# A sparse 3x3 convolution on one core: all cast loads queued at the start, fixed output tiles

## The chip, the cores and the metric

The kernel runs on one core of a Trainium2 chip. The metric is the device time of one execution in microseconds, the median of several runs. The core has five engines that matter here: TensorE (PE) multiplies, VectorE (DVE), ScalarE (ACT) and GpSimd (POOL) work on tiles, and SyncE (SP) issues transfers. Transfers run on 16 DMA engines. Those that SP issues stand in queue q1, those that POOL issues in queue q0.

## The reference

The input `x` has 16 images of 64 channels with 64 x 64 points, the weight has 128 output channels, 64 input channels and 3 x 3 taps, about 90% of them zero. All data are 32-bit floats. What is computed is an ordinary convolution with a border of zeros:

```python
x_pad = np.pad(x, ((0, 0), (0, 0), (pad, pad), (pad, pad)), mode='constant')
output = np.zeros((batch, c_out, h, w), dtype=np.float32)
for b, co, ci, kh, kw in ...:
    if weight[co, ci, kh, kw] != 0:
        output[b, co] += weight[co, ci, kh, kw] * x_pad[b, ci, kh:kh+h, kw:kw+w]
```

The output is 33.55 MB, twice the 16.78 MB of `x`.

## The kernel before

The zeros are not used; the kernel is dense. Two images make a pair: their 2 x 64 channels fill the 128 partitions, and PE runs the two images' matmuls on the two halves of its rows (K = 64 each). There are eight pairs, p = 0 to 7, and eight input tiles `xs[p]` in bf16, all in SBUF for the whole run, so no load ever waits for a buffer.

**Loads.** The weight and the first half of pair 0 (`x_head`) come as plain 32-bit loads on SP's queue; casts on DVE and ACT make bf16 of them. All other input comes through POOL's queue as DMAs that cast to bf16 while they move (`load`, L68, and L63 for the second half of pair 0). Pairs 1 to 3 and the first 24 rows of pair 4 are issued at the start (`EARLY`, `CUT`). The rest is issued later: after the last block of pairs 1 to 5 the program issues, in turn, the rest of pair 4, pair 5, pair 6, and pair 7 in two halves (`LATER`). Since POOL works its instructions off in order, such a load goes out when POOL has done the `s` of that block.

**Compute.** A pair has four blocks of 16 rows. All blocks but the first of pair 0 go through `twos`: POOL adds neighbouring rows into a tile `s` (L169), PE makes a product `shared` from it, ACT copies that from PSUM to `pc` (L176), PE makes a product for the even and one for the odd rows (L150), and DVE adds `pc` to each of them and writes `o` (L183, four writes of 128 x 512 a block). The first block of pair 0 goes through `direct`. Each of PE's products takes two tiles of the PSUM pool, which has eight, one bank each.

**Stores.** The output of a pair is one tile `both` of 4 MB, from a pool with three buffers (`bufs=3`); `o[0]` and `o[1]` are its two images. When a pair is done, SP issues one store for it (L207). Pair 7 goes out in two stores, after block 1 and after block 3 (L205). DVE's first write of pair p + 3 waits until the store of pair p has landed, because it takes that buffer. After the store of pair 1, SP issues five loads of one number each into a tile `spare` (L211), which nothing reads. DMAs of SP take eight semaphores in turn; before a DMA takes a semaphore again, SP waits for the DMA that had it before. With the five small ones, pair 3's store follows pair 0's on the same semaphore, pair 4's follows pair 1's, and pairs 5 to 7 follow the small ones.

The program fixes the order of every engine's instructions as written (`manual_schedule`).

Of the kernel before, what the change touches and what calls it, by code (L numbers as in the profile page):

```python
# [8 lines left out]
FP32 = mybir.dt.float32  # L9
# [2 lines left out]
SUB = mybir.AluOpType.subtract  # L12

BLOCKS = {p: "TTTT" for p in range(8)}
BLOCKS[0] = "DTTT"  # L20


G0, G1, G2, G21, G01 = range(5)
# [4 lines left out]
def kernel(  # L28
# [6 lines left out]
    nc = tc.nc  # L35

    B, C_IN, H, W = x.shape
    C_OUT, _, KH, KW = weight.shape
    assert (B, C_IN, H, W) == (16, 64, 64, 64) and (C_OUT, KH, KW) == (128, 3, 3)
    NP = B // 2  # L40
    HEAD = 32

    const_pool = ctx.enter_context(tc.tile_pool(name="const", bufs=1))
    x_pool = ctx.enter_context(tc.tile_pool(name="x", bufs=1))
    s_pool = ctx.enter_context(tc.tile_pool(name="s", bufs=3))
    p_pool = ctx.enter_context(tc.tile_pool(name="pc", bufs=4))
    o_pool = ctx.enter_context(tc.tile_pool(name="o", bufs=3))
    psum_pool = ctx.enter_context(
        tc.tile_pool(name="psum", bufs=8, space=bass.MemoryType.PSUM)
    )  # L50
# [4 lines left out]
    def pair(p):  # L55
        return x[2 * p : 2 * p + 2].rearrange("n i h w -> (n i) h w")

    xs = [x_pool.tile([128, H, W], BF16, name=f"x{p}") for p in range(NP)]
# [5 lines left out]
    ident = const_pool.tile([128, 128], BF16, name="ident")  # L64
    make_identity(nc, ident)

    def load(p, a=0, b=H):
        nc.gpsimd.dma_start(out=xs[p][:, a:b, :], in_=pair(p)[:, a:b, :])  # L68

    EARLY, CUT = 4, 24

    LATER = {2: (5,), 3: (6,), 4: (7, 0, 32), 5: (7, 32, 64)}
    for p in range(1, EARLY):
        load(p)
    load(EARLY, 0, CUT)


    idle_rhs = const_pool.tile([128, 512], BF16, name="idle_rhs")  # L80
    nc.vector.memset(idle_rhs, 0.0)  # L81
# [2 lines left out]
    def keep_busy(n):  # L84
        for _ in range(n):
            nc.tensor.matmul(idle_ps, idle_rhs[:, 0:128], idle_rhs, start=True, stop=True)  # L86

    keep_busy(7)

    w_v = w_sb.rearrange("o (i k) -> o k i", k=KH * KW)
# [66 lines left out]
    def direct(p, o, r0, rows):  # L159
        ps = product(  # L160
            [(xs[p], G1, r0, 1), (xs[p], G0, r0 - 1, 1), (xs[p], G2, r0 + 1, 1)], rows
        )
        nc.scalar.copy(out=o[0][:, r0 : r0 + rows, :], in_=ps[0])  # L163
        nc.vector.tensor_copy(out=o[1][:, r0 : r0 + rows, :], in_=ps[1])  # L164

    def twos(p, o, r0):
        t0 = r0 // 2
        s = s_pool.tile([128, 8, W], BF16, name="s")
        nc.gpsimd.tensor_tensor(  # L169
            out=s, in0=xs[p][:, r0 : r0 + 16 : 2, :], in1=xs[p][:, r0 + 1 : r0 + 16 : 2, :], op=ADD  # L170
        )
        shared = product([(s, G1, 0, 1)], 8)
        pc = []
        for n in range(2):
            c = p_pool.tile([128, 8, W], FP32, name="pc")
            nc.scalar.copy(out=c, in_=shared[n])  # L176
            pc.append(c)
        even = [(xs[p], G21, r0 + 1, 2), (xs[p], G0, r0 - 1, 2)]
        odd = [(xs[p], G01, r0, 2), (xs[p], G2, r0 + 2, 2)]
        for first, terms in ((r0, even), (r0 + 1, odd)):  # L180
            ps = product(terms, 8)
            for n in range(2):
                nc.vector.tensor_tensor(  # L183
                    out=o[n][:, first : r0 + 16 : 2, :], in0=ps[n], in1=pc[n], op=ADD
                )

    for p in range(NP):
        both = o_pool.tile([C_OUT, 2, H, W], FP32, name="o")
        o = [both[:, n] for n in range(2)]
        into = out[2 * p : 2 * p + 2].rearrange("n o h w -> o n h w")  # L190
        last = p == NP - 1
        for blk in range(4):
            r0 = 16 * blk
            if BLOCKS[p][blk] == "T":
                twos(p, o, r0)
                if p == 1 and blk == 3:
                    load(EARLY, CUT, H)
                elif blk == 3 and p in LATER:
                    load(*LATER[p])
            else:  # L200
                for r, rows in ((r0, 8), (r0 + 8, 8)):
                    direct(p, o, r, rows)
            if last and blk % 2 == 1:
                rows = slice(r0 - 16, r0 + 16)
                nc.sync.dma_start(out=into[:, :, rows, :], in_=both[:, :, rows, :])  # L205
        if not last:
            nc.sync.dma_start(out=into, in_=both)  # L207
        if p == 1:
            spare = const_pool.tile([1, 5], FP32, name="spare")
            for k in range(5):  # L210
                nc.sync.dma_start(out=spare[:, k : k + 1], in_=weight[0:1, 0, 0, 0:1])  # L211


# [28 lines left out]
```

## Time and profile before

| what | value |
|---|---|
| time, median of 3 runs | 126.25 us (125.86 to 126.41) |
| span of the profiled execution | 124.3 us (no time beside the span is given for it; the median of the runs is 1.95 us above it) |
| PE | 108.7 us busy, 87% |
| DVE | 82.5 us busy, 66% |
| POOL | 41.7 us busy, 34% |
| ACT | 39.0 us busy, 31% |
| read from HBM, written to HBM | 17.07 MB, 33.55 MB |
| DMA queues, share of 16 engines | q1 67.2%, q0 30.7% |
| mean granted PE clock | 0.956 |

The span runs from the first to the last instruction. A DMA view counts what a cast load writes, two bytes a number, though it reads four; so a stretch with loads alone shows half of the rate that it reads. Packets are what a DMA engine moves at a time: here one row of one partition, 16 KB of 32-bit numbers at most. "Landing" is when the semaphore of a DMA has got its full count. A line of the timeline gives start, duration, engine, line, operation, tiles, number, and in brackets how long the engine was idle before it and what ended that.

### The profile page before, as it was taken

To read this page: it belongs to the slowest core of one execution; us is meant where nothing else is said; L and a number is where in the kernel's file an instruction comes from. 1 tells how busy PE (TensorE), PEld (TensorE's weight loads), DVE (VectorE), ACT (ScalarE), POOL (GpSimd) and SP (SyncE) were. 2 spreads that over 40 slices of the span, in tenths; PEclk is the share of its full clock that TensorE was granted. 3 is DMA by queue.
4 is the path that set the end of the run, shared out by engine and by line. 5 is a ranking of instruction groups with operands and counts; after the bars stand their busy time and mean duration, and the time that the engine had idled before them with its cause. 6 is when DMAs were issued, how large, how long until landed. Compare 5 with 4: busy or idle time off the path is not lost.

```text
span 124.3 us, 2453 instructions
## 1 busy us (share of the span) xinstructions
PE 108.7 (87%) x989; PEld 57.2 (46%) x989; DVE 82.5 (66%) x135; ACT 39.0 (31%) x71; POOL 41.7 (34%) x47
## 2 busy tenths in 40 slices
PE   6959999999999999999999999999999999970000
PEld 2425555555555555555555555555555555530000
DVE  0353577877787778777877878887877787772000
ACT  4543333333333333333333333333333333330000
POOL 6409333533353335333443335333333320000000
PEclk9999999999999999999999999999999999997555
DMA  4999999999999999999999999999999999999991
GB/s 120 348 220 227 219 213 213 238 411 338 335 392 422 319 316 324 377 340 329 303 385 378 354 380 443 376 349 389 418 422 437 422 427 427 437 427 403 432 414 82
DMA packets 4198, 42.91 MB, mean 345 GB/s; under 512 B 347, under 2 KB 347, under 8 KB 1115
## 3 DMA queue, kind: packets, MB, share of 16 engines
q1 hardware_dynamic: 2746, 34.90, 67.2%
q0 software_dynamic: 1440, 7.86, 30.7%
q8 instruction: 7, 0.11, 0.3%
q14 instruction: 5, 0.03, 0.1%
HBM read 17.07 MB, written 33.55 MB: 407 GB/s over the span
## 4 chain that ended last, share of the span: by engine, by line
PE 82%; DMA 5%; DVE 1%; issue 1%; DVEq 0%; SPq 0%
PE ps L150 82%; DMA x_head<-in_x_dram 5%; DVE o L183 1%; DVEq L237 0%; DVE x L101 0%; SPq L60 0%; DVEq L183 0%
## 5 line engine op out<-in xcount | busy, mean ns | idle before, releaser
L183 DVE TENSOR_TENSOR o<-ps,pc 128x512 f32<-128x512 f32 x124 | 77.8, 686 | 22.1 <-PE ps L150 19.2
L150 PE MATMUL ps<-x,wT 64*128 64x504 bf16 (+3 forms) x780 | 88.8, 373 | 1.3 <-DVE x L101 1.3
L150 PEld LDWEIGHTS <-wT 64*128 64x128 bf16 x966 | 55.2, 94 | 49.5 <-issue 1.7
L169 POOL TENSOR_TENSOR s<-x 128x512 bf16<-128x512 bf16 x31 | 35.6, 1150 | 57.6 <-PE ps L150 41.1
L176 ACT COPY pc<-ps 128x512 f32<-128x512 f32 x62 | 33.3, 589 | 64.0 <-issue 61.8
L150 PE MATMUL ps<-s,wT 64*128 64x512 bf16 (+1 forms) x186 | 25.7, 377 | 0.0
L86 PE MATMUL ps<-idle_rhs 128*128 128x512 bf16 x14 | 4.8, 505 | 1.2 <-DVE idle_rhs L81 1.2
L68 POOL DMA_DIRECT2D x<-in_x_dram x9 | 5.0, 560 | 0.0
L86 PEld LDWEIGHTS <-idle_rhs 128*128 128x128 bf16 x14 | 1.5, 118 | 3.2 <-issue 1.4
L105 DVE CAST w_bf<-w_sb 128x192 bf16<-128x192 f32 (+1 forms) x4 | 1.1, 351 | 2.5 <-DMA w_sb<-in_weight_dram 2.5
L164 DVE COPY o<-ps 128x512 f32<-128x512 f32 x2 | 1.4, 692 | 2.0 <-PE ps L150 2.0
L101 DVE CAST x<-x_head 128x576 bf16<-128x576 f32 x1 | 0.5, 460 | 2.6 <-DMA x_head<-in_x_dram 2.6
L101 ACT CAST x<-x_head 128x576 bf16<-128x576 f32 (+1 forms) x2 | 1.5, 802 | 1.8 <-DMA x_head<-in_x_dram 1.8
L163 ACT COPY o<-ps 128x512 f32<-128x512 f32 x2 | 1.2, 586 | 2.4 <-PE ps L150 2.4
L105 ACT ACT_TABLE_LOAD x1 | 1.3, 1283 | 0.7 <-PEq L226 0.7
L105 ACT CAST w_bf<-w_sb 128x64 bf16<-128x64 f32 (+1 forms) x2 | 0.7, 416 | 1.6 <-DMA w_sb<-in_weight_dram 1.6
L115 DVE TENSOR_TENSOR wT<-ps,wT 128x384 bf16<-128x384 f32 x2 | 1.0, 548 | 0.0
L111 PEld LDWEIGHTS <-w_bf 128*128 128x128 bf16 x9 | 0.5, 97 | 1.0 <-DVE w_bf L105 1.0
L63 POOL DMA_DIRECT2D x<-in_x_dram x1 | 0.7, 693 | 0.8 <-POOLq L226 0.8
L111 PE MATMUL ps<-ident,w_bf 128*128 128x128 bf16 x9 | 0.9, 222 | 0.1
L81 DVE MEMSET idle_rhs<- 128x256 uint32 x1 | 0.3, 272 | 0.9 <-PEq L226 0.9
L126 DVE CAST wT<-ps 128x384 bf16<-128x384 f32 x1 | 0.6, 551 | 0.0
(8 smaller groups left out, 1.9 us busy)
## 6 DMA issues: line engine op xcount, KB each, us to landing
out_dram<-o SPq DMA_DIRECT2D x7, 4096.0 KB, 19.8
x<-in_x_dram POOLq DMA_DIRECT2D x5, 1024.0 KB, 16.8
out_dram<-o SPq DMA_DIRECT2D x2, 2048.0 KB
x<-in_x_dram POOLq DMA_DIRECT2D x3, 512.0 KB, 13.8
x_head<-in_x_dram SPq DMA_DIRECT2D x1, 1024.0 KB, 6.2
x<-in_x_dram POOLq DMA_DIRECT2D x1, 640.0 KB, 14.8
x<-in_x_dram POOLq DMA_DIRECT2D x1, 384.0 KB, 22.3
w_sb<-in_weight_dram SPq DMA_DIRECT2D x1, 288.0 KB
```

What stands on the lines that cost most here:

```text
L68: nc.gpsimd.dma_start(out=xs[p][:, a:b, :], in_=pair(p)[:, a:b, :])
L86: nc.tensor.matmul(idle_ps, idle_rhs[:, 0:128], idle_rhs, start=True, stop=True)
L101: copy(out=xs[0][:, a:b, :], in_=x_head[:, a:b, :])
L105: copy(out=w_bf4[:, g, a:b, :], in_=w_v[:, k : k + b - a, :])
L111: nc.tensor.matmul(wps[:, j, :], src, ident, start=True, stop=True)
L115: nc.vector.tensor_tensor(out=wT[:, g], in0=wps, in1=wT[:, G1], op=SUB)
L150: nc.tensor.matmul(ps[n][:, lo:hi, c_lo:c_hi], tap(g, kw, n), src[q, a:b:step, c_lo + kw - 1 : c_hi + kw - 1], start=(i == 0), stop=(i == ...
L163: nc.scalar.copy(out=o[0][:, r0 : r0 + rows, :], in_=ps[0])
L164: nc.vector.tensor_copy(out=o[1][:, r0 : r0 + rows, :], in_=ps[1])
L169: nc.gpsimd.tensor_tensor(out=s, in0=xs[p][:, r0 : r0 + 16 : 2, :], in1=xs[p][:, r0 + 1 : r0 + 16 : 2, :], op=ADD)
L176: nc.scalar.copy(out=c, in_=shared[n])
L183: nc.vector.tensor_tensor(out=o[n][:, first : r0 + 16 : 2, :], in0=ps[n], in1=pc[n], op=ADD)
```

## The change

The loads of pairs 1 to 7 are all issued at the start, each whole, in the order of the pairs. `load`, `EARLY`, `CUT`, `LATER` and the issues between the blocks go. The output pool gets one buffer for each of three tiles with names of their own, made once before the loop, and pair p writes tile p % 3. Waits on these tiles come from the regions that instructions write and read, where before they came from a buffer that is given back and taken again. Which pairs are stored in halves, and the number of small loads, become constants with the values they had.

```diff
+HALVES = (7,)
+SPARES = 5
...
-    o_pool = ctx.enter_context(tc.tile_pool(name="o", bufs=3))
+    o_pool = ctx.enter_context(tc.tile_pool(name="o", bufs=1))
...
-    def load(p, a=0, b=H):
-        nc.gpsimd.dma_start(out=xs[p][:, a:b, :], in_=pair(p)[:, a:b, :])
-    EARLY, CUT = 4, 24
-    LATER = {2: (5,), 3: (6,), 4: (7, 0, 32), 5: (7, 32, 64)}
-    for p in range(1, EARLY):
-        load(p)
-    load(EARLY, 0, CUT)
+    for p in range(1, NP):
+        nc.gpsimd.dma_start(out=xs[p], in_=pair(p))
...
+    outs = [o_pool.tile([C_OUT, 2, H, W], FP32, name=f"o{k}") for k in range(3)]
     for p in range(NP):
-        both = o_pool.tile([C_OUT, 2, H, W], FP32, name="o")
+        both = outs[p % 3]
...
                 twos(p, o, r0)
-                if p == 1 and blk == 3:
-                    load(EARLY, CUT, H)
-                elif blk == 3 and p in LATER:
-                    load(*LATER[p])
...
-            if last and blk % 2 == 1:
+            if p in HALVES and blk % 2 == 1:
...
-        if not last:
+        if p not in HALVES:
             nc.sync.dma_start(out=into, in_=both)
         if p == 1:
-            spare = const_pool.tile([1, 5], FP32, name="spare")
-            for k in range(5):
+            spare = const_pool.tile([1, SPARES], FP32, name="spare")
+            for k in range(SPARES):
```

More of the change, by code (lines that the diff above doesn't have):

```diff
@@ L185, in twos @@
                 )
+    outs = [o_pool.tile([C_OUT, 2, H, W], FP32, name=f"o{k}") for k in range(3)]
     for p in range(NP):
-        both = o_pool.tile([C_OUT, 2, H, W], FP32, name="o")
+        both = outs[p % 3]
         o = [both[:, n] for n in range(2)]
         into = out[2 * p : 2 * p + 2].rearrange("n o h w -> o n h w")
-        last = p == NP - 1
         for blk in range(4):
```

## The prediction

> **What bounds the kernel now.** I read the page first, parts 2 and 3, then the chain that ended last, then the DMA view of single stretches, then DVE's and POOL's timelines. Part 2 has two rows near their top (each digit is a fortieth of the span, 3.1 us):
>
> ```profile
> PEclk9999999999999999999999999999999999997555
> DMA  4999999999999999999999999999999999999991
> ...
> q1 hardware_dynamic: 2746, 34.90, 67.2%
> q0 software_dynamic: 1440, 7.86, 30.7%
> ```
>
> PE ends at 111 us (slice 36). The DMA row has no low slice from the second to the last but one. Part 3 says the same in numbers: q1 (the stores and the two plain loads, from SP) took 67.2% of 16 engines' span, q0 (the cast loads, from POOL) 30.7%. With 0.4% of instruction fetches that is 98.3% of 124.3 us, or 122.2 us of full work; the missing 2.1 us are mostly the first 1.8 us and the end. The chain shows another picture:
>
> ```profile
> 7.95 102.09 PE ps L150 x954
> ...
> 111.99 0.60 DVE o L183
> ```
>
> It ends at DVE's last write, 112.6, because the store issued then has nothing behind it. What follows is a transfer, and its place shows in the DMA view from 112.6 to the end:
>
> ```profile
> DMA packets 509, 3.87 MB, mean 331 GB/s; under 512 B 36, under 2 KB 36, under 8 KB 36
> ```
>
> The last store is 2048 KB, 2.10 MB. So 1.77 MB of older stores stood before it. At the 427 GB/s of the last full slices that is 4.1 us. The first packet of a store comes 1.3 us after its issue (first store: issued 23.03, first q1 packet record 24.31). So PE and DVE could end 2.8 us later, by the mean engine, before the queue runs dry: that is the slack of the compute. For the slowest engine (the store before lands at 118.2, 4.3 us after 113.9) it is about 4 us. The DMA engines are the bound, and PE has 2.8 to 4 us in hand.
>
> **The change, part by part.** The bytes are the same. If the DMA engines always have work, an order alone cannot move the end; only cheaper packets or an empty queue can.
>
> *Fewer, longer packets.* A load of a pair is 128 packets, 8 per engine. In the packet records a 16 KB source row landing as 8192 bytes takes 626 ns, a half (4096) 324, the two pieces of pair 4 (3072 and 5120) 250 and 400. Pair 4 whole instead of cut: 8 x (250 + 400 - 626) = 0.19 us per engine. Pair 7 whole instead of halved: 8 x (2 x 324 - 626) = 0.18 us. Sum: 0.37 us.
>
> *Loads beside stores.* Store packets of 16 KB take 614 ns alone (88 to 112 us), 624 beside whole loads (42 to 62), 621 to 625 beside half loads and 640 beside pair 4's pieces (28 to 36). Packets alternate one for one (below), so loads in pieces put 6 x 8 = 48 store packets per engine beside a load, whole loads 4 x 8 = 32. Before: 16 x 26 + 16 x 10 + 16 x 9 = 0.72 us over the 614; after: 32 x 10 = 0.32 us. Sum: 0.40 us. Packet times overlap a little (shares of 101 to 103%), so this is an upper value. Moved bytes by stretch (loads at their source size) give 425 GB/s in full mixture and 429 without: 27.97 MB moved from 24 to 90 us would take 65.6 us instead of 66, which is 0.4 us for both terms together. Ends: 0.77 and 0.38 us. If all mixing ran as at 28 to 36 us, the 16 ns more for 32 packets would cost 0.5 us, and the gain would fall to about 0. I take 0.45 us, nearer to the moved bytes, since those don't count overlap.
>
> *Issue on POOL.* Loads 4b, 5, 6, 7a, 7b go from behind the last `s` of pairs 1 to 5 to the front. There POOL has room:
>
> ```profile
> 2.46 2.15 POOL L68 DMA_DIRECT2D x<-in_x_dram  x4
> 9.04 2.26 POOL L169 TENSOR_TENSOR s<-x 128x512 bf16<-128x512 bf16 x2 [4.43 <-ACT x L101]
> ```
>
> Seven issues of 0.55 us end at 6.3 instead of 4.6; the first `s` waits for ACT's cast until 9.04. The cover is 2.7 us, the cost nothing. Without that cover each issue would move `s` by 0.55 us. The five issues that vanish later lie in POOL's idle time.
>
> *No lead between issue and data.* The single loads begin about 4.4 us after their issue (24.07 to 28.45), during which stores run alone at full rate; queued loads follow without a gap:
>
> ```profile
> q0 software_dynamic: 418, 3.01, 103.2%
> ```
>
> That is the stretch 8 to 22 us with loads alone: full. So a DMA fewer saves no fixed time here, 0 us. The Trainium skill, "DMA: Bandwidth & Descriptors", section "Anatomy of one DMA", gives each such DMA about 2.0 us of fixed time; two fewer would by that be an estimated 4.0 us and a median of 122.2, but the full stretch speaks against it.
>
> *Stores land later; DVE waits.* This is the step that matters for PE. When both queues hold work they share:
>
> ```profile
> q1 hardware_dynamic: 105, 1.72, 51.2%
> q0 software_dynamic: 99, 0.81, 48.6%
> ```
>
> (42 to 50 us.) One load packet, one store packet. At 24.3 us pair 3 is in; pairs 4 to 7 are 32 packets per engine. Alternating, a pair of packets takes 1.25 us, times 0.985 for the overlap 1.23. Store 0 (16 packets) ends at 24.3 + 19.7 = 44, store 1 and the loads at about 63.6; from there 9.8 us a store: store 2 at 73.4, store 3 at 83. The same reckoning on the kernel before gives its landings 0.5 to 1.6 us early (39.1 against 40.0, 53.8 against 55.4), so 45, 65, 74.8, 84.5 are to be expected. A pair's first DVE write needs the store three pairs back, with the pool as with the fixed tiles:
>
> ```profile
> out_dram<-o SPq DMA_DIRECT2D x1, 4096.0 KB, 19.6
> ...
> 49.14 2.53 DVE L183 TENSOR_TENSOR o<-ps,pc 128x512 f32<-128x512 f32 x4 [0.58 <-ACT pc L176]
> ...
> 61.95 2.53 DVE L183 TENSOR_TENSOR o<-ps,pc 128x512 f32<-128x512 f32 x4 [0.58 <-ACT pc L176]
> 74.75 1.93 DVE L183 TENSOR_TENSOR o<-ps,pc 128x512 f32<-128x512 f32 x3 [0.58 <-ACT pc L176]
> ```
>
> (First line: store 1, issued 35.78, landed 55.4.) Pair 3 at 49.14 has 4 us left, pair 4 at 61.95 misses store 1 by 3.0 us, pair 5 meets store 2. Behind the waiting write stand DVE's other writes alone; PE waits for the PSUM banks that they free. PE has eight banks and uses six a block: after the even rows (61.9) it can do the odd rows, the next shared product and the next even rows, some 3 us, to about 64.95. The first bank comes free at 65 + 0.68, the second at 66.4, so PE loses 1.0 to 1.4 us. DVE then gains 0.7 us a block (2.52 busy in 3.24). PE's end moves from 111.1 to 112.4, inside the slack of 2.8. On the end: 0. Without the slack it would be 1.2 us more. SP's queue waits for store 1 only before store 4 (74.2): no cost.
>
> *Fixed tiles with regions.* Same three buffers, same bytes, same whole-pair wait, pair 7 in two halves as before: 0. If a region were taken for the whole tile, pair 7's lower half would wait for the upper half's store, 106.2 to about 118: that is a rival below.
>
> Sum: span 124.3 - 0.45 = 123.85. The median of the runs, 126.25, stands 1.95 us above the profiled span; that stays. 126.25 - 0.45 = 125.8 us.
>
> **The rivals.** B, slower: *the loads take more than half of the shared engines.* With two load packets to a store packet, store 0 ends at 24.3 + 16 x 1.85 = 53.9, lands at 55 and DVE stands 5.8 us at pair 3; PE, with 2.4 us of cover, loses 3.4. Such a hole can also drop PE's clock: after the last matmul (111.1) the granted clock is
>
> ```profile
> 113.00:115.00 2.00, 0.00 (x0) 0.00 (x0) 0.00 (x0) 0.00 (x0) 0.00 (x0) 0.62 1.02 434
> ```
>
> 0.62 in this stretch and 0.50 in the next: it fell about 2.4 us after PE stopped. How fast it returns no row shows; between nothing and as long again at half speed I take the latter, 1.2 us. PE is then 4.6 us late, 0.6 to 1.8 beyond the slack. It decides from 2.8 us of lost PE time; the median would be 126.4 to 127.8, taken as 127.0. For it: every later wait hangs on store 0. Against it: the 51.2 to 48.6 of the shared stretch. The Trainium skill, "TensorE: Matmul & The Clock Gate", Part 1, speaks against a change that lets PE wait for transfers: one idle window of about 3.4 us halves the clock. By that rule the 1.2 us hole of my forecast leaves the clock alone, and the hole of B would be just long enough.
>
> C, slower: *POOL is held when more loads are queued than the five of before.* If the last three issues had to wait until xs0's half and pairs 1 and 2 had landed (19.3), the first `s` would come 10 us late, less the 4 us slack: 132. Against it: five issues at an even 0.55 us. The same price, up to 134, if a region is tracked as the whole tile.
>
> D, no change: *the shorter packets' extra time overlaps elsewhere* and the order is neutral: 126.2, within 126.0 and 126.5. For it: shares above 100%.
>
> E, faster: *both packet terms count in full*, 0.77 us, and the gaps around restarted loads add to it: 125.3.
>
> **How the numbers follow.** The forecast A (125.8; its own range 125.2 to 126.9, the upper end if mixing costs as at 28 to 36 us and PE's delay uses up the slack) gets 0.62, B 0.17, C 0.06, D 0.10, E 0.05. A difference of 0.5%, 0.63 us, is about what a measurement of this kernel can tell from none: faster is below 125.6, slower above 126.9. Faster: 0.22 of A and E, 0.27. Same: 0.35 of A, D, 0.03 of B, 0.48. Slower: 0.05 of A, 0.14 of B, C, 0.25. The range 125.2 to 127.4 leaves out C, the upper part of B and some of E.
>
> **What would show it.** Right: the DMA row full to the end; loads landing until about 63 us; a wait of DVE for `out_dram<-o` of some 3 us near 62, PE short of work for about 1 us near 65; last store issued near 113.9; packets of q0 down from 1440 to 1152. Wrong: a low slice in the DMA row, a DVE wait at 49, a PEclk below 9 inside the loop, or an `s` later than 9.1.

## The result, and the profile after

The changed kernel takes 127.62 us in the median of 4 runs (127.31 to 127.94), against 126.19 us (125.86 to 126.41, 4 runs) for the kernel before. The ratio is 1.0114, with a 95% interval of 1.0079 to 1.0149: it is slower by 1.4 us, where 125.8 us was forecast. Some executions of the same kernel take over 1.5% longer than its fastest; the ratios here and below leave them out, and so differ a little from the quotient of the medians. The profiled execution took 127.94 us, its span 125.5 us.

**The page.** The same rows as before (part 2, then part 3):

```profile
PEclk9999999999999999999999999999999999998555
DMA  4999999999999999999999999999999999999980
GB/s 94 368 225 214 219 214 212 214 196 342 313 324 332 319 300 339 329 329 316 394 423 428 433 439 433 423 418 426 433 433 439 415 418 428 433 410 428 426 376 21
...
q1 hardware_dynamic: 2746, 34.90, 66.2%
q0 software_dynamic: 1152, 7.86, 30.7%
```

The DMA row is still full from the second slice to slice 38. Only the last two slices differ: 8 and 0, where they were 9 and 1. By this row alone nothing happened. The GB/s row says more, at slice 9 (25 to 28 us): 196, the lowest of the loop. q0 has 288 packets fewer, as the two loads that are no longer cut should give.

**The chain.** Start, duration, engine and line of the pieces that ended last:

```profile
8.29 57.15 PE ps L138 x534
65.44 0.68 DVE o L171
66.12 0.04 issue
66.16 44.88 PE ps L138 x406
...
113.02 0.60 DVEq L221
```

One piece of PE has become two, with a write of DVE between them at 65.4. The end of DVE's work has moved from 112.6 to 113.6. DVE's and PE's timelines around that place (the bracket is the idle time before, and what ended it):

```profile
49.48 2.53 DVE L171 TENSOR_TENSOR o<-ps,pc 128x512 f32<-128x512 f32 x4 [0.58 <-PE ps L138]
...
64.82 1.29 DVE L171 TENSOR_TENSOR o<-ps,pc 128x512 f32<-128x512 f32 x2 [3.12 <-ACT pc L164]
```

```profile
63.97 1.96 PE L138 MATMUL ps<-x,wT 64*128 64x512 bf16 x13
66.16 1.45 PE L138 MATMUL ps<-x,wT 64*128 64x512 bf16 x11 [0.23 <-DVE o L171]
```

DVE stands 3.1 us before pair 4's first write. The bracket names ACT, which had been done for long; what ended the wait is store 1, whose landing is in the issue rows of the DMA view (KB, us from issue to landing):

```profile
out_dram<-o SPq DMA_DIRECT2D x1, 4096.0 KB, 25.0
...
out_dram<-o SPq DMA_DIRECT2D x1, 4096.0 KB, 28.6
```

Store 0 is issued at 23.37 and lands at 48.3; store 1 is issued at 36.11 and lands at 64.7.

**Where the time is lost.** Windows of 4 us, the kernel after (the last three columns are granted clock, DMA share and GB/s):

```profile
24.00:28.00 4.00, 4.00 (x41) 2.11 (x38) 3.27 (x6) 1.07 (x2) 1.16 (x1) 1.00 0.97 178
28.00:32.00 4.00, 4.00 (x40) 2.09 (x38) 3.27 (x6) 1.07 (x2) 1.15 (x1) 1.00 1.05 344
```

and the kernel before:

```profile
24.00:28.00 4.00, 4.00 (x40) 2.09 (x38) 3.27 (x6) 1.07 (x2) 1.21 (x2) 1.00 1.06 397
```

The GB/s column counts a cast load at half of what it reads, so 178 against 397 exaggerates. With the packet records (loads at the size of their source, each packet by its part in the stretch) 24 to 28 us moves 346 GB/s after and 420 before; 24 to 32 us moves 3.06 MB against 3.32 MB. At 0.43 MB per us that is 0.6 us of all 16 engines, though the share says 0.97: the engines are busy, on packets that take longer. From 20 to 25 us a load packet takes 625 ns; from 25 to 27.5, with store 0 issued and not yet moving, the load packets take 870 ns in the mean and up to 1248. Store 0's first packet comes at 27.41, 4.04 us after its issue; before it came after 1.28 us.

**The end.** Each DMA engine closes a store with a small packet of its own. In the packet records those of the last store end at 121.89 in the mean of the engines and at 122.99 for the last one before, at 122.31 and 124.14 after. So 1.15 us came at the end of the packets: 0.42 in the mean, and 0.73 because the last engine lags more, 1.83 us instead of 1.10. After the change one engine ends 1.3 us behind the second last; before they are 0.1 us apart. The same closing packets exist for every store, and they show when the lag arises (last engine behind the mean of the 16, us; pair 7 has two stores):

| kernel | store 3 | store 4 | store 5 | store 6 | store 7, first half | second half |
|---|---|---|---|---|---|---|
| before | 2.19 | 1.20 | 1.08 | 1.10 | 1.10 | 1.10 |
| after | 0.93 | 0.99 | 1.44 | 1.87 | 1.86 | 1.83 |

It grows during stores 5 and 6, long after the entry of store 0, and stands still in the last two.

### The profile page after: what moved, and what is told of

Read it like the earlier page. It is cut to its first block, busy times and chain, and to the rows that moved or that the text cites. A ratio compares the mean times of both kernels' runs of the same rounds, so it can differ in the third digit from the quotient of the medians.

```text
span 125.5 us, 2489 instructions
## 1 busy us (share of the span) xinstructions
PE 109.6 (87%) x989; PEld 57.0 (45%) x989; DVE 82.1 (65%) x135; ACT 39.0 (31%) x71; POOL 40.7 (32%) x45
## 3 DMA queue, kind: packets, MB, share of 16 engines
q0 software_dynamic: 1152, 7.86, 30.7%
## 4 chain that ended last, share of the span: by engine, by line
PE 81%; DMA 5%; DVE 2%; issue 1%; DVEq 1%; SPq 0%
PE ps L138 81%; DMA x_head<-in_x_dram 5%; DVE o L171 2%; DVEq L221 0%; DVE x L89 0%; SPq L59 0%; DVEq L171 0%
## 5 line engine op out<-in xcount | busy, mean ns | idle before, releaser
L138 PE MATMUL ps<-x,wT 64*128 64x504 bf16 (+3 forms) x780 | 91.8, 373 | 1.2 <-DVE x L89 0.8
L164 ACT COPY pc<-ps 128x512 f32<-128x512 f32 x62 | 33.3, 589 | 64.7 <-issue 57.5
L138 PE MATMUL ps<-s,wT 64*128 64x512 bf16 (+1 forms) x186 | 28.2, 377 | 0.0
L67 POOL DMA_DIRECT2D x<-in_x_dram x7 | 3.7, 561 | 0.0
L62 POOL DMA_DIRECT2D x<-in_x_dram x1 | 0.7, 696 | 0.8 <-POOLq L210 0.8
L112 ACT CAST wT<-ps 128x384 bf16<-128x384 f32 x1 | 0.5, 478 | 0.4 <-PE ps L99 0.4
```

Of the source, the lines that this page charges most:

```text
L67: nc.gpsimd.dma_start(out=xs[p], in_=pair(p))
L138: nc.tensor.matmul(ps[n][:, lo:hi, c_lo:c_hi], tap(g, kw, n), src[q, a:b:step, c_lo + kw - 1 : c_hi + kw - 1], start=(i == 0), stop=(i == ...
```

## The experiments

Three theories were open. H: store 0, entering while whole loads stand in the other queue, slows everything for some us. W: DVE's wait at pair 4, which makes later stores later. L: one DMA engine is slower on stores that have no load beside them, and the change leaves more such stores. T, the fixed tiles, was the rival that had nothing to do with transfers. Every ratio is against the kernel before on the same chip, with its 95% interval. "Mean", "last" and "lag" are those of the last store's closing packets.

**1. The tiles alone, and the loads alone.** The kernel before with the three fixed tiles:

```diff
-    o_pool = ctx.enter_context(tc.tile_pool(name="o", bufs=3))
+    o_pool = ctx.enter_context(tc.tile_pool(name="o", bufs=1))
+    outs = [o_pool.tile([C_OUT, 2, H, W], FP32, name=f"o{k}") for k in range(3)]
...
-        both = o_pool.tile([C_OUT, 2, H, W], FP32, name="o")
+        both = outs[p % 3]
```

> The kernel before with the three fixed output tiles; its loads stay as they were. H (the DMA engines lose time when store 0 meets the queue of whole loads), W (DVE's wait for store 1 puts the last store later) and L (one slow DMA engine gets more store packets without a load beside them) all put the loss on the loads: 126.2 us. T (the tiles bring the waits): 127.6 us.

125.86 against 125.87 us, ratio 0.9987 [0.9958, 1.0017]. The tiles cost nothing. (Of this kernel only the times are used.) The reverse, the kernel after with its tiles put back into the pool of three:

```diff
-        both = outs[p % 3]
+        both = o_pool.tile([C_OUT, 2, H, W], FP32, name="o")
```

> The changed kernel with the output pool of three buffers; all loads are still issued at the start. H, W and L: 127.6 us, with the poor stretch from 24 to 28 us and DVE's 3 us wait as in the changed kernel. T: 126.2 us.

127.02 against 125.87, 1.0086 [1.0059, 1.0114]. The loads carry the loss. Its profile repeats all three marks: store 0's first packet 4.34 us after its issue, 2.94 MB from 24 to 32 us, last 124.16 with a lag of 1.84. T is out.

**2. When the loads are issued.** No load of pair 4 at the start, each later load whole, one pair at a time:

```diff
-    LATER = {2: (5,), 3: (6,), 4: (7, 0, 32), 5: (7, 32, 64)}
+    LATER = {1: (4,), 2: (5,), 3: (6,), 4: (7,)}
-    load(EARLY, 0, CUT)
...
-                if p == 1 and blk == 3:
-                    load(EARLY, CUT, H)
```

> The kernel before with pairs 4 to 7 loaded whole, one each behind the last block of pairs 1 to 4; only pairs 1 to 3 at the start, so that store 0 finds the load queue run out, and no store is late. H and W: neither loss, and the packet saving of 0.4 us is left, 125.8 us. L: as many store packets without a load beside them as in the changed kernel, so the slowest engine's last landing lies some 1.9 us behind the mean (1.2 before) and the time is about 126.5.

127.40, 1.0113 [1.007, 1.0156]: as slow as the change, with no load queued behind store 0 and no DVE wait of note (0.73 us at most from 46 to 70 us). Neither expectation held: the lag is 1.22, and the loss lies in the mean, 123.01. The windows of this kernel show why:

```profile
22.00:24.00 2.00, 2.00 (x22) 1.12 (x20) 1.40 (x3) 0.86 (x2) 1.55 (x2) 1.00 0.67 205
24.00:27.00 3.00, 3.00 (x32) 1.60 (x28) 2.27 (x5) 1.07 (x2) 1.14 (x1) 1.00 1.06 437
27.00:29.00 2.00, 2.00 (x22) 1.03 (x18) 1.79 (x3) 0.81 (x2) 0.71 (x1) 1.00 1.03 254
```

First the load queue ran dry just before store 0 (share 0.67). Then store 0, issued at 22.52 with nothing beside it, came fast (first packet 0.92 us later, 437 GB/s). Then pair 4's load entered, and 27 to 29 us fell to 254 GB/s at a share of 1.03. This column counts loads at half; with loads at the size of their source it is 281 GB/s, between 416 from 24 to 27 us and 404 from 29 to 32. So it isn't the load queue as such: a queue that begins beside a busy one costs, whichever of the two is new.

The next kernel issues pairs 1 to 4 whole at the start and the others one at a time as before:

```diff
-    EARLY, CUT = 4, 24
+    EARLY = 5
-    LATER = {2: (5,), 3: (6,), 4: (7, 0, 32), 5: (7, 32, 64)}
+    LATER = {2: (5,), 3: (6,), 4: (7,)}
```

> Pairs 1 to 4 whole at the start, pairs 5 to 7 whole behind the last blocks of pairs 2 to 4. Store 0 meets one whole load, nothing deeper; stores land in time. H: if a whole load beside the first store is enough, the poor stretch at 24 to 28 us is there and costs 0.6 us, 126.4; if it takes a deep queue, 125.8. W: no wait, 125.8. L: 126.5.

126.72, 1.0046 [1.0021, 1.007]. One whole load behind store 0 is enough for H: first packet 4.28 us after the issue, 336 GB/s from 24 to 28 us. DVE doesn't wait at 61.5, so it gives back W and keeps H; mean 121.99, lag 1.55.

**3. Shorter packets beside store 0.** The kernel after with pair 4 cut at row 24, still all at the start:

```diff
-        nc.gpsimd.dma_start(out=xs[p], in_=pair(p))
+        for a, b in ((0, 24), (24, H)) if p == 4 else ((0, H),):
+            nc.gpsimd.dma_start(out=xs[p][:, a:b, :], in_=pair(p)[:, a:b, :])
```

> The changed kernel, all loads at the start, but pair 4 in its old two pieces (24 and 40 rows), so that store 0 meets short load packets (250 ns) where it met whole ones (626 ns); DVE still waits for store 1. The new kernel stands 1.2 to 1.4 us above the kernel before. H in the form 'the first store's start is dear when the other queue's packets are long': the poor stretch at 24 to 28 us goes, the first store packet comes within 1.5 us of the issue, and 0.6 us come back less 0.2 us for the shorter packets: 0.8 to 1.0 us above before. H in the form 'a deep queue is dear': nothing changes, 1.2 to 1.4 above. W: the DVE wait is still there, 1.2 to 1.4 above.

127.47, 1.0122 [1.0077, 1.0167], first packet 4.70 us after the issue, 301 GB/s from 24 to 28 us. H in the form "it is the long packets" falls. DVE's wait was longer, and here the bracket names the store:

```profile
65.51 4.88 DVE L172 TENSOR_TENSOR o<-ps,pc 128x512 f32<-128x512 f32 x8 [4.78 <-DMA out_dram<-o]
```

The kernel before with 40 rows of pair 4 at the start instead of 24:

```diff
-    EARLY, CUT = 4, 24
+    EARLY, CUT = 4, 40
```

> The kernel before with the cut of pair 4 after 40 rows in place of 24: when store 0 is issued, the load queue holds some 4.3 us of work where it held 3.0, and 6 us where pairs 1 to 4 went whole. H as a matter of how much is queued: the first store packet comes 1.3 to 4 us after its issue and 0.1 to 0.6 us are lost; as an all-or-nothing matter, either the 1.3 us of before or about 4 us and the full 0.6. L and W: no change. So 0 to 0.6 us above before.

126.27, 1.0026 [0.9999, 1.0053]. Here too store 0's first packet comes late, 3.85 us after its issue, and 24 to 32 us moves 2.99 MB. The mark appears between 24 and 40 rows and hardly grows with more. In the profiled execution the mean is 122.45, 0.56 later than before. Its time (126.94) stands above the median, so of the time only the interval is used: it allows anything from nothing to 0.7 us.

**4. What a late PE costs.** The kernel before with more matmuls into a spare bank before pair 4, 6 and 22 of them:

```diff
         last = p == NP - 1
+        if p == 4:
+            more_ps = psum_pool.tile([128, 512], FP32, name="ps")
+            for _ in range(6):
+                nc.tensor.matmul(more_ps, idle_rhs[:, 0:128], idle_rhs, start=True, stop=True)
```

> The kernel before with six idle matmuls (512 columns, about 0.22 us each) ahead of pair 4, which make PE, DVE and the last store about 1.3 us late, as DVE's wait does in the changed kernel; the transfers stay. H and L, and my forecast (2.8 us of slack): the time of before within 0.2 us. W: 1.0 to 1.4 us above before.

> The same with 22 idle matmuls, about 4.8 us. By a slack of 2.8 to 4 us: 0.8 to 2.0 us above before, so that the slack has an end where it was put. W (every microsecond counts): 4.8 us above.

Six: 126.66 against 126.13, 1.0037 [1.0008, 1.0065], +0.5 us. Twenty-two: 130.09, 1.0329 [1.0285, 1.0373], +4.0 us. The matmuls themselves take 1.3 and 4.8 us of PE's time; from the issue of store 3 to that of the last store it is 1.5 and 5.0 us longer than before. So in both cases about 1.0 us is free, not 2.8 to 4. The windows of the longer delay show the place:

```profile
100.00:104.00 4.00, 4.00 (x42) 1.83 (x40) 3.27 (x6) 1.30 (x3) 1.29 (x2) 1.00 0.66 274
104.00:108.00 4.00, 4.00 (x42) 1.83 (x40) 2.94 (x5) 1.91 (x4) 1.02 (x1) 1.00 0.78 328
```

The store queue runs dry here, not at the end: store 5 was issued at 91.64 and store 6, a whole pair, only at 104.44. In the kernel before the engines close store 5 from 101.4 to 103.4, at 102.3 in the mean, and store 6 is issued at 99.81; with the 1.28 us from issue to first packet of store 0 it could begin at an estimated 101.1, 1.2 us ahead of the mean. The 1.77 MB ahead of the last store said nothing of this.

**5. Stores in halves.** The kernel after with pairs 4 to 7 stored in halves (8 KB packets instead of 16 KB):

```diff
-HALVES = (7,)
+HALVES = (4, 5, 6, 7)
```

> The changed kernel with pairs 4 to 7 stored in halves, as pair 7 alone was: store packets of 8 KB in the stretch where only stores run. In the trace of the changed kernel one DMA engine takes 644 to 660 ns for a 16 KB store packet there and the others 611, while 8 KB packets take 309 on all. L: the last landing comes back from 1.9 to about 1.2 us behind the mean, the time falls by 0.7 us, to 0.5 to 0.7 above before. H and W: 1.2 to 1.4 us above before as in the changed kernel.

127.50, 1.0125 [1.008, 1.0171], mean 122.32, lag 1.73. While PE works, the slow engine is as slow on 8 KB packets: 94 of them together take 1.8 us more than the others' do, nearly all before PE's last matmul ends (112.49). Smaller stores don't mend L. The 309 ns "on all" of the expectation are those of the last stores, which mostly run when PE has stopped; even in the kernel after only 420 of 512 take them (510 before). Pair 0 in halves, so that the first store comes 7 us earlier, deep in the loads:

```diff
-HALVES = (7,)
+HALVES = (0, 7)
```

> The changed kernel with pair 0 stored in halves, so that the first store comes about 6 us earlier and meets pair 2's and 3's loads. H as 'the entry of the first store': the poor stretch moves with it to about 18 to 20 us and is as costly (0.6 us). H as 'something at 25 us': it stays at 25. W: stores start 6 us earlier, store 1 lands at about 59, DVE doesn't wait for it at 62, and the last store is issued 0.7 to 1.0 us earlier; if W costs much, this kernel gains that over the changed one (1.2 to 1.4 us above before becomes 0.4); by the two delays just measured (about 0.8 us are free) it gains 0.1 to 0.3 only. L: store packets beside loads as in the changed kernel, the lag of the last engine stays at 1.7 to 1.9 us.

127.73, 1.0129 [1.0096, 1.0163]. The poor stretch moved with the first store (issued 16.36, first packet 3.80 us later): 393 and 390 GB/s from 16 to 24 us, and 3.38 MB from 24 to 32 us, more than before the change. H goes with the first store's entry, not with a place in the program. Nothing is gained: the half lands after 19.7 us, and DVE still waits 3.9 us at pair 4:

```profile
65.08 5.47 DVE L171 TENSOR_TENSOR o<-ps,pc 128x512 f32<-128x512 f32 x9 [3.94 <-DMA out_dram<-o]
```

**6. Loads in halves.** The kernel before, with pairs 5 and 6 also loaded in halves, puts more store packets beside a load:

```diff
                     load(EARLY, CUT, H)
+                elif blk == 3 and p in (2, 3):
+                    load(p + 3, 0, 32)
+                    load(p + 3, 32, 64)
```

> The kernel before with pairs 5 and 6 loaded in halves too, both halves issued at the old place: 16 load packets more per engine, 0.36 us of dearer packets. L: more store packets lie beside a load (38 of 112 per engine now, 52 or so then), the slow engine has fewer slow packets (72 now, about 58 then) and ends 0.5 us less behind the mean, so the time is that of before within 0.2 us, rather lower. Without L: 0.3 to 0.4 us above before.

126.57, 1.0037 [1.0009, 1.0064]; the profiled execution is the fastest of them, 125.93 (they reach up to 127.58). L's part came as expected: 54 slow store packets where 58 were expected, and a lag of 0.67 instead of 1.10. The median doesn't show it: it is 0.5 us slower than before, more as expected without L. The profile shows a small loss (419 and 402 GB/s from 44 to 52 us, where before moves 423 and 428), but it is that of the fastest execution, so it doesn't explain the median. The kernel after with pairs 4 to 7 loaded in halves, all at the start:

```diff
-        nc.gpsimd.dma_start(out=xs[p], in_=pair(p))
+        for a, b in ((0, 32), (32, H)) if p >= 4 else ((0, H),):
+            nc.gpsimd.dma_start(out=xs[p][:, a:b, :], in_=pair(p)[:, a:b, :])
```

> All loads at the start as in the changed kernel, but pairs 4 to 7 in halves each: 0.72 us of dearer packets against the changed kernel, 0.36 against before. Load packets are half as long, so the loads' share beside the stores falls to a third, store 1 lands before 61 and DVE doesn't wait (W gone); some 50 of 112 store packets per engine lie beside loads (L: about 60 slow packets, lag near 1.2). H is left (0.6 us). H + L: the loss of the changed kernel becomes 0.6 to 0.9 us above before. W alone: 0.36 above. H alone (no L): 1.2 or more.

139.94, 1.1089 [1.1055, 1.1123], far from every expectation, for a reason outside the theories. Its POOL timeline:

```profile
2.47 3.73 POOL L68 DMA_DIRECT2D x<-in_x_dram  x7
9.10 0.53 POOL L68 DMA_DIRECT2D x<-in_x_dram  x1 [2.90 <-DMA x<-in_x_dram]
13.98 0.53 POOL L68 DMA_DIRECT2D x<-in_x_dram  x1 [4.35 <-DMA x<-in_x_dram]
...
24.25 4.46 POOL L158 TENSOR_TENSOR s<-x 128x512 bf16<-128x512 bf16 x4
```

Twelve loads are four too many: after the eighth, POOL holds each issue until an earlier load has landed, and the first `s` comes at 24.25 instead of 9.4. The trace names what holds them: POOL's loads take eight semaphores in turn, and each of the four comes 0.28 us after the landing of the load eight places ahead, which had the same semaphore (8.82, 13.70, 18.56, 23.42). This kernel says nothing of W or L. It shows what rival C described, beyond eight loads; the change has exactly eight.

**7. H and W taken away, L kept.** The loads stay as before up to pair 4; then, after pair 1, pairs 5 to 7 are issued whole in one go, and run through beside the stores:

```diff
                     load(EARLY, CUT, H)
-                elif blk == 3 and p in LATER:
-                    load(*LATER[p])
+                    for later in (5, 6, 7):
+                        load(later)
```

> The kernel before up to store 0 (pairs 1 to 3 and 24 rows of pair 4 at the start); all other loads are issued in one go behind the last s of pair 1, pairs 5 to 7 whole, and run through beside the stores. H is taken away (store 0 finds the load queue nearly empty, first packet within 2 us, no poor stretch at 25), W too (store 1 lands near 60). L stays: some 84 slow packets, lag 1.6 to 1.8 us. H and L: mean end of the last store 121.7 to 122.0, last packet 123.5, the time 0.4 to 0.7 us above before. H alone: the time of before or 0.2 less. L alone: 1.0 to 1.2 above.

126.49 against 125.99, 1.0045 [1.0013, 1.0077]. Store 0's first packet comes 1.77 us after its issue, 24 to 32 us moves 3.34 MB, DVE doesn't wait, and the last store is issued at 112.31. The windows show the stretch that the change had lost:

```profile
24.00:28.00 4.00, 4.00 (x41) 2.10 (x38) 3.27 (x6) 1.07 (x2) 2.54 (x4) 1.00 1.08 403
```

and DVE's first write of pair 4:

```profile
61.65 2.53 DVE L183 TENSOR_TENSOR o<-ps,pc 128x512 f32<-128x512 f32 x4 [0.58 <-PE ps L150]
```

The mean is back (121.79), the lag isn't (1.55). This is what H and L together expected: 0.4 to 0.7 us stay. The same with those loads in halves:

```diff
+                    for later in (5, 6, 7):
+                        load(later, 0, 32)
+                        load(later, 32, 64)
```

> The same with pairs 5 to 7 in halves: 0.54 us of dearer load packets against e13, one and a half times as many load packets beside the stores. L: 60 to 66 slow packets, lag 0.8 to 1.1 us, so that the mean end rises by 0.4 to 0.5 and the last packet doesn't: the time of e13 or up to 0.3 less. Without L: 0.4 to 0.5 above e13.

126.80, 1.0058 [1.0021, 1.0096]. The lag fell to 0.86, as L expected, but with 90 slow packets and not 60 to 66, and the mean rose to 122.74 (394, 381 and 401 GB/s from 24 to 28, 28 to 32 and 36 to 40 us). What the lag gave back was lost there.

No version was faster than the kernel before.

**L in numbers.** In the packet records a 16 KB store packet takes 611 ns where no load is beside it, but a small group takes longer, mostly 634 to 660; beside whole loads nearly all take 624. Slow is here what takes over 622 and under 680 ns, without those 624. Over the whole span 72 are slow before (2.42 us above 611 in all) and 86 after (3.01 us). After the last load, when nothing is mixed, their number is mostly close to the number of store packets that one single engine carries there, and the lag goes roughly with it:

| kernel (experiment) | slow after the last load | one engine's store packets there | slow in all | lag, us |
|---|---|---|---|---|
| pairs 5, 6 in halves (6) | 35 | 38 | 54 | 0.67 |
| before | 36 | 37 | 72 | 1.10 |
| 40 rows of pair 4 (3) | 39 | 42 | 62 | 1.14 |
| burst in halves (7) | 49 | 46 | 90 | 0.86 |
| 6 more matmuls (4) | 49 | 36 | 87 | 1.32 |
| each pair's load staged (2) | 53 | 59 | 78 | 1.22 |
| pairs 1 to 4 at the start (2) | 55 | 58 | 76 | 1.55 |
| 22 more matmuls (4) | 61 | 29 | 114 | 1.56 |
| burst (7) | 75 | 71 | 84 | 1.55 |
| after | 83 | 81 | 86 | 1.83 |
| the loads alone (1) | 85 | 82 | 88 | 1.84 |
| pair 4 cut (3) | 87 | 77 | 89 | 1.70 |
| pair 0 stored in halves (5) | 99 | 86 | 99 | 1.73 |

The order isn't perfect: the two kernels with a late PE have more slow packets than one engine carries, and the burst in halves has many slow packets among its loads (41, of all lengths from 627 to 676 ns) with a small lag. The kernel with twelve loads (6), which the table leaves out, has 226 slow packets after its last load where one engine carries 106, and a lag of 0.09; its store queue runs dry between the stores.

The records carry no engine's number, but while a queue is full a packet starts 3 to 4 ns before the one ahead of it on its engine ends, so they can be strung together. Back from the last closing packet of store 6, the chain of the kernel after (closing at 114.33) has 76 packets of 16 KB from 65.5 us on, 73 of them over 630 ns. Before (closing at 113.19) it has 37 such packets among 38 from 88.8 us on. So in both it is one engine, and the one that ends the program. With pairs 5 and 6 in halves this engine closes store 6 at 112.69 and another is last, at 112.77: there the lag no longer measures it. With 22 more matmuls and with twelve loads slow packets also run side by side (34 of 54 and 109 of 182 over 630 ns overlap another by 0.3 us or more), so more than one engine is slow there.

The chain of slow packets has an end, too. In all fifteen profiles that are used here its last one begins no earlier than 1.1 us before PE's last matmul ends, and at most 0.1 us after it (before: 111.31 and 111.23; after: 112.46 and 112.44); single ones come up to 1.9 us later. That fits the lag, which stands still in the last two stores. So the slowness belongs to stores with no load beside them while the compute engines work. POOL is not what it hangs on: before, its last work ends at 100.4.

## Why the prediction was wrong, step by step

**Right.** Fewer packets (q0 1152). The loads land until 62.8 us (63 forecast). Whole loads and stores share one for one: from 42 to 50 us the trace of after has 113 packets of q0 and 111 of q1 (16 of them closing packets). DVE waits 3.1 us before 64.8 (3.0 forecast). The last store is issued at 113.64 (113.9 forecast), 1.03 us later than before; 0.33 of that came with the head (below), so PE lost about 0.7 us where 1.0 to 1.4 were forecast. POOL's seven issues cost nothing:

```profile
2.47 3.73 POOL L67 DMA_DIRECT2D x<-in_x_dram  x7
9.37 3.36 POOL L157 TENSOR_TENSOR s<-x 128x512 bf16<-128x512 bf16 x3 [3.17 <-ACT x L89]
```

The first `s` still waits for ACT; it is 0.3 us later because `x_head` landed at 7.75 instead of 7.42, which is no part of the change that I can name. The fixed tiles cost nothing (experiment 1). The saving of fewer packets and cleaner mixing was taken as 0.45 us: from 32 to 112 us the engines moved 0.14 MB more than before, 0.3 us. Two DMAs fewer gave no 4.0 us, so the trace's full stretch was rightly preferred to the fixed time per DMA of the Trainium skill, "DMA: Bandwidth & Descriptors", section "Anatomy of one DMA"; queued transfers don't pay it one after the other here.

**Wrong, the first step that failed: "If the DMA engines always have work, an order alone cannot move the end."** The engines always had work, and the order moved the end. Busy is not the same as moving: from 24 to 28 us the share is 0.97 and the bytes are 18% down. The rows that I took the entry of a store from showed it beside the last pieces of a short load, where its first packet comes 1.3 us after the issue. I used this 1.3 us for a store that enters beside a full load queue, and gave the entry itself no price. Measured: 4.04 us, and 0.6 us lost to all engines. A price stood in the prediction's own row: of the 126 store packets from 28 to 36 us before, 115 take 624 ns in the mean; the 640 that I read as the price of short pieces comes from 11 packets of 684 to 1025 ns, nine of them between 28.08 and 28.45 us, just ahead of the first packet of load 4b. It is the entry of a queue. Nor did the stores run "at full rate" while load 4b was on its way: from 26.4 to 28.5 us the kernel before moves 404 GB/s, and 382 from 40.6 to 41.8 us, where load 5 enters. Store 0 started at 27.4 and not at 24.3, and landed at 48.3 where 45 was forecast; store 1's landing (64.7 against 65) came out right by luck, for while store 0 stood still the loads went on, and fewer of them were left beside store 1.

**Wrong, the term that was not in the sum: the slowest engine.** The prediction reckoned the end "by the mean engine". The program ends with the last one, and it lagged 0.73 us more. The step that failed is the half of *Loads beside stores* that priced a store packet alone at 614 ns against 624 beside a load, and so found fewer mixed packets a gain. For most of the engines that holds (611 against 624). For one it is the other way until PE stops, 634 to 660 against 624, and this one ends the program. Fourteen more slow packets are 0.59 us (3.01 - 2.42), most of the 0.73; the rest of it I can't place. Experiments 6 and 7 moved the lag with the number of such packets after the last load, down (35 packets, 0.67) and up (75, 1.55); the burst in halves (49, 0.86) doesn't follow the order.

**Wrong, but without a price here: "PE has 2.8 to 4 us in hand."** It has about 1.0 (experiment 4; the expectations after it worked with 0.8). The smallest backlog of the store queue is where the last whole pair is issued, near 100 us, not at the end. In the changed kernel PE's delay of 0.7 us should have cost little, as it is within the 1.0 and the transfers themselves were late by then: from 100 to 104 us it moves 430 GB/s by the windows, as much as its neighbours. No run takes DVE's wait away and leaves the rest, so its price is argued, not measured. If "On the end: 0" was right, it was by a wrong reason.

**The sum by the measured terms,** at the last store's closing packets: entry of store 0 +0.60, the head +0.12 (0.05 MB fewer by 8 us, tied to `x_head`'s landing in this one execution), cheaper packets -0.32: +0.40, where the mean shows +0.42 (121.89 to 122.31). The lag +0.73. Together +1.15; the span grew by 1.2, the medians differ by 1.43. What is left of the median, about 0.2, lies within the spread of the runs. Experiment 7 checks the split: without H and W the ratio falls from 1.0114 to 1.0045, and the last packet comes at 123.33, 0.8 us earlier, with the lag still at 1.55.

**The rivals.** B had the sign and nearly the size (127.0), by another mechanism: the loads did not take more than half, and there was no wait at 49. The clock part of B can be read off experiment 6's twelve loads. After the change, PE's short hole near 66 us (0.23 us idle in the timeline) left the clock at 1.00, which tests nothing. In the kernel with twelve loads PE stood for 14.14 us, from 11.32 to 25.46: the granted clock fell 5.1 us after the stop, and came back 4.6 us after PE began again. The Trainium skill, "TensorE: Matmul & The Clock Gate", Part 1, has windows of about 3.4 us that run freely; a fall after 2.2 and 2.5 us (the ends of the kernels before and after) and after 5.1 us, and a return after 4.6 us, lie on both sides of one such window and within two. The page asks for an idle window before a fall; here 2.2 us without a matmul were enough once, and in another kernel 5 were needed, so the length of a hole alone does not decide. The 1.2 us that I took for the return in B were too few: 4.6 us at half speed are 2.3 us. C did not occur at eight loads, and did at twelve. D and E are out.

**Open.** Why a queue that begins beside a busy one makes the other's packets slower for about 2.4 us, and why 24 rows of pair 4 avoid it where 40 do not: its occurrence, place and size are shown, not its cause. Not every entry costs: before, none is seen where loads 6, 7a and 7b begin. Why one engine is slower on stores alone while PE works, and which of the 16 it is: the chain of its packets is shown, not its cause or its number. The split of the 1.4 us into entry and lag rests on packet records of single profiled executions; the runs that bear it out each moved one of the two, but other terms of some 0.1 to 0.4 us moved with them.

## What to carry to other kernels

A full DMA row says that engines are busy, not that they move bytes: compare bytes per stretch, loads at the size of their source, before an order of transfers is called neutral. Price the entry of a new queue beside a busy one by a row in which just that happens, and reckon the end by the slowest engine's packets, not by the mean. Work out slack at every issue of a store, where the backlog is smallest, and not at the end alone.

## What the runs showed of the hardware that I had not expected

- A first store beside cast loads that go on behind it: 3.63 to 4.70 us from issue to first packet in eight kernels, 1.2 to 1.9 us beside the last pieces of a short load (six kernels); after the change the load packets go from 625 to as much as 1248 ns until it starts. A load that enters beside a running store can do the same to it (281 GB/s for 2 us in experiment 2, loads at the size of their source).
- Before and after the change one of the 16 DMA engines is 4 to 8% slower on stores (634 to 660 ns against 611), only until PE's last matmul, and not beside cast loads (624 on nearly all). The Trainium skill, "DMA: Bandwidth & Descriptors", section "Latency and other measured facts", says that two of the engines are usually slower and guesses at the software queue's descriptors. Here it is one in these two kernels and more in two others, they are slow where no load of that queue is left, and as fast as the others where one runs beside them: if it is the same slowness, the runs speak against that cause.
- POOL's issues of more than eight loads wait for earlier landings, with 2.90 to 4.35 us of POOL standing each time; work queued behind them on POOL stands too (PE idle 14.14 us). This comes from the program's eight semaphores (experiment 6); whether the chip would take more, no run shows.
